# The first loads of an encoder kernel, cut in another way and in another order

## The chip, the cores and the metric

The kernel runs on one core of one Trainium2 chip. The metric is the time on the device in microseconds (us) of one execution. Before the change it is 922.29 us, the median of three runs (920.82 to 923.38).

The engines are named as in the profile: PE multiplies matrices (PEld loads its stationary operand), DVE and ACT work on vectors, POOL does small work, SP issues the transfers from memory. Each engine takes its instructions strictly in the order of its own queue.

## The reference

Two layers of an encoder for 256 rows (`SEQ`) of 1024 columns, in float32. The start of the first layer is all that the change touches:

```python
u = rms_norm(h, g_mix_pre)                       # h is the input x in layer 0
(gq, gk, gv, gg, ra_f, ra_b, aq, ak, av, gate_a, gate_b) = jnp.split(u @ w_in, offsets, axis=-1)
```

The rest of a layer is gated linear attention, grouped-query attention with rotary positions, a merge of both, a SwiGLU block and an embedding. The first columns that the kernel multiplies are the 32 decay ranks (`ra_f`, `ra_b`) and the 1024 of `aq`, which lie side by side in `w_in`: 1056 columns.

## The kernel before

**Numbers in two parts.** Each operand is cut into a high part (a copy in the format that PE takes at full rate) and the low remainder. A product is three matmuls: high by high, low by high, and high by the remainder of the weights. ACT makes the high part of a weight by a copy, DVE makes the remainder by a subtraction.

**K-tiles.** The 1024 columns of x are eight k-tiles of 128. For each, PE turns x (a transpose of 128x128 for each half of the rows, `turn`), then a high part (`high` on ACT or `high_here` on DVE) and a low part (`rest` on DVE) are made, scaled with the gain column `gcol`. The 1056 columns of weights are cut into 288, 384 and 384 (`RQ`), and each of these three and each half of the rows has its own accumulator: 18 matmuls for one k-tile. `rq_first` (the first four k-tiles, whose matmuls have line 105 in the profile) and `rq_step` (the others, line 121) issue them. For the very first k-tile the order is by column group, both halves in turn: four matmuls on the first 288 columns, four on the next 384, four on the last 384, then the six with the remainders of the weights.

**Loads.** SP issues x in pieces (`load_x`) and the weights by a list (`plan`, carried out by `Stream.load`). One load of the list holds two k-tiles, and there are two buffers for such loads; a load into a buffer waits until DVE has made the last remainder from it. `FIRST` says how the first two loads are cut: k-tile 0 as 288 and 768 columns, k-tile 1 whole, then k-tiles 2 and 3 whole. The order on SP is: x columns 0 to 256, the 288, the 768, k-tile 1, x columns 256 to 512, k-tiles 2 and 3, x columns 512 to 1024. The load of k-tiles 4 and 5 follows when its buffer is free, and behind it six small transfers of the decay weights (`up_weights`).

**The start.** `start()` is a generator that writes out the order by hand: `on(engine, ...)` chains its instructions on each engine, and `yield n` hands over to the matmuls for n steps (`tick`). In the kernel before, it turns k-tiles 0 and 1 of both halves (four transposes), issues two warm-up matmuls (`WARM[2]`), makes the high parts of k-tile 0 on DVE, then weights and low parts of k-tiles 0 and 1, and yields 5 steps before the turns of k-tiles 2 and 3. Work outside this list (line 774: ACT's copy of the decay weights, line 129: DVE's subtraction for it) is placed by a scheduler. Before any of it, PE runs six narrow and three wide warm-up matmuls (`WARM[0]`, `WARM[1]`) on constants.

In the profile all that `on` issues has line 142.

Of the kernel before, what the change touches and what calls it, by code (L numbers as in the profile page):

```python
# [48 lines left out]
UNIT = 2112  # L49
RQ = ((0, 288), (288, 672), (672, 1056))  # L50

WARM = 6, 3, 2

FIRST = ((0, 0, 288), (0, 288, 1056), (1, 0, 1056)), ((0, 0, 1056), (1, 0, 1056))
C_GQ, C_GK, C_GV, C_GG, C_RA = 0, 512, 1024, 2048, 3072
C_AQ, C_AK, C_GA, C_GB = 3104, 4128, 4640, 5664

# [2 lines left out]
def trunk_kernel(ctx: ExitStack, tc: tile.TileContext, a: dict, out: bass.AP):  # L60
# [21 lines left out]
    def nm(s):  # L82
        uid[0] += 1
        return f"{s}_{part[0]}_{uid[0]}"
# [10 lines left out]
    def aux():  # L95
        return accp.tile([P, 512], F32, tag="acc", name=nm("aux"))
# [7 lines left out]
    def mm(o, lhsT, rhs, start, stop):  # L104
        return nc.tensor.matmul(o, lhsT, rhs, start=start, stop=stop)  # L105

    def mm3(o, l, r, start, stop):
        (lh, ll), (rh, rl) = l, r
        mm(o, lh, rh, start, False)
        mm(o, lh, rl, False, False)  # L110
        mm(o, ll, rh, False, stop)
# [27 lines left out]
    def on(e, f, *args, **kw):  # L139

        with tc.issue_after(line[e].ins) if e in line else nullcontext():
            line[e] = f(*args, **kw)
# [9 lines left out]
    def load_x(c0, c1):  # L152
        on("dma", nc.sync.dma_start, h[:, :, c0:c1], a["x"][0, :, c0:c1].rearrange("(s p) c -> p s c", p=P))

    load_x(0, 256)
    on("act", nc.scalar.dma_start, grow, a["g_mix_pre"][0].rearrange("(k p) -> k p", p=P))


# [29 lines left out]
    def unit_rows(w, n, c0=0, c1=D, parts=None):  # L188

        if parts:  # L190

            return lambda t: [
                (t[:, k * (c1 - c0) + x : k * (c1 - c0) + y], w[(2 * n + k) * P : (2 * n + k + 1) * P, c0 + x : c0 + y])
                for k, x, y in parts
            ]
        return lambda t: [
            (
                t[:, : 2 * (c1 - c0)].rearrange("p (k c) -> p k c", k=2),
                w[n * 256 : (n + 1) * 256, c0:c1].rearrange("(k p) c -> p k c", p=P),
            )  # L200
        ]

    plan = []
    for l in range(DEPTH):
        w = a["w_in"][l]
        plan += [unit_rows(w, n, C_RA, C_RA + 1056, FIRST[n] if l == 0 and n < 2 else None) for n in range(4)]
        for c0 in (C_AK, C_GQ, C_GK, C_GV, C_GV + 512, C_GG, C_GG + 512):
# [25 lines left out]
    class Load:  # L233
# [5 lines left out]
        def start(self):  # L239
            if self.own:  # L240
                self.raw = self.own()
            else:
                self.raw = rawp.tile([P, UNIT], F32, tag="raw", name=nm("raw"))
            return self.make(self.raw)

    class Stream:
# [33 lines left out]
                self.lend = False  # L280
            return wp.tile([P, UNIT], F32R, tag=tag, name=nm("lent")).bitcast(F32)

        def load(self):

            self.room += 1
            self.start()

        def start(self):
            while self.loads and (self.lend or not self.loads[0].waits) and (self.loads[0].own or self.room):
                x = self.loads.pop(0)  # L290
                self.room -= not x.own
                moves = x.start()
                for dst, src in moves:
                    if self.open:
                        nc.sync.dma_start(dst, src)
                    else:
                        on("dma", nc.sync.dma_start, dst, src)
                x.n = sum(math.prod(dst.shape[1:]) for dst, _ in moves)
# [66 lines left out]
    ws = Stream(4)  # L365
# [410 lines left out]
        return wup  # L776


    ws.load()
    load_x(256, 512)  # L780
    ws.load()
    load_x(512, 1024)
    unit_a, unit_b = ws.pieces()
# [3 lines left out]
    def warm_up(n, wide=False):  # L787

        x = keep if wide else seed
        for _ in range(n):  # L790
            on("pe", mm, warm[:, 0 : x.shape[-1]], seed, x, True, True)

    warm_up(WARM[0])
    warm_up(WARM[1], True)
    uT = Split()
# [9 lines left out]
    def square_here(hf, j):  # L805
        on("dve", nc.vector.scalar_tensor_tensor, out=t512(), in0=hv(hf, j), scalar=1.0 / 1024.0, in1=hv(hf, j),
           op0=ALU.mult, op1=ALU.mult, accum_out=ss[hf][:, j : j + 1])

    def square(hf, j):
        on("act", nc.scalar.activation, t512(), hv(hf, j), AF.Square, scale=1.0 / 32.0, accum_out=ss[hf][:, j : j + 1])  # L810

    def rstd(hf):
        on("pool", nc.gpsimd.tensor_scalar,
           out=rs[hf], in0=ss[hf][:, 0:1], scalar1=ss[hf][:, 1:2], scalar2=EPS, op0=ALU.add, op1=ALU.add)
        on("pool", nc.gpsimd.tensor_scalar, out=he[hf], in0=rs[hf], scalar1=P * EPS, scalar2=None, op0=ALU.mult)
        on("pool", nc.gpsimd.tensor_tensor, out=rs[hf], in0=rs[hf], in1=neghalf[:, 0:1], op=ALU.pow)
        last_pow[0] = line["pool"]
# [10 lines left out]
    def gains():  # L828

        ps = aux()  # L830
        on("pe", nc.tensor.transpose, ps[:, 0:8], grow, ident[0:8, 0:8])
        on("dve", nc.vector.tensor_copy, gcol, ps[:, 0:8])

    def low(hi, lo, src):
        on("dve", nc.vector.tensor_tensor, out=lo, in0=src, in1=hi.bitcast(F32), op=ALU.subtract)

    def split_here(hi, lo, src):
        on("act", nc.scalar.copy, hi, src)
        low(hi, lo, src)
# [3 lines left out]
    def turn(hf, *ks):  # L843

        if (hf, ks[0] // 4) not in banks:
            banks[hf, ks[0] // 4] = aux()
        for k in ks:
            ps = banks[hf, k // 4][:, k % 4 * P : (k % 4 + 1) * P]
            on("pe", nc.tensor.transpose, ps, h[:, hf, k * P : (k + 1) * P], ident)

    def high(hf, *ks):

        for k in ks:
            ps = banks[hf, k // 4][:, k % 4 * P : (k % 4 + 1) * P]
            on("act", nc.scalar.activation, uT.at(k, 1, hf * P, P)[0][:, 0, :], ps, AF.Copy, bias=0.0, scale=gcol[:, k : k + 1])

    def high_here(hf, k):

        ps = banks[hf, k // 4][:, k % 4 * P : (k % 4 + 1) * P]
        hi = uT.at(k, 1, hf * P, P)[0][:, 0, :]  # L860
        on("dve", nc.vector.tensor_scalar, out=hi, in0=ps, scalar1=gcol[:, k : k + 1], scalar2=None, op0=ALU.mult)

    def rest(hf, *ks):

        for k in ks:
            ps = banks[hf, k // 4][:, k % 4 * P : (k % 4 + 1) * P]
            hi, lo = (t[:, 0, :] for t in uT.at(k, 1, hf * P, P))
            on("dve", nc.vector.scalar_tensor_tensor, out=lo, in0=ps, scalar=gcol[:, k : k + 1],
               in1=hi.bitcast(F32), op0=ALU.mult, op1=ALU.subtract)

    def start():
        cut = lambda piece, c: [t[:, c] for t in piece]

        def split_cut(piece):
            for c in RQ:
                on("act", nc.scalar.copy, *(t[:, slice(*c)] for t in piece[::2]))

        gains()
        for k in range(2):
            for hf in range(2):  # L880
                turn(hf, k)
        warm_up(WARM[2])
        for hf in range(2):
            high_here(hf, 0)
        split_cut(unit_a)
        rest(0, 0)
        rest(1, 0)
        low(*cut(unit_a, slice(0, 288)))
        for hf in range(2):
            high_here(hf, 1)  # L890
        low(*cut(unit_a, slice(288, 1056)))
        split_cut(unit_b)
        rest(0, 1)
        rest(1, 1)
        low(*cut(unit_b, slice(0, 288)))
        low(*cut(unit_b, slice(288, 1056)))
        ws.load()
        unit_c, unit_d = ws.pieces()
        yield 5
        turn(0, 2, 3)  # L900
        high(0, 2, 3)
        rest(0, 2, 3)
        split_here(*unit_c)
        yield 1
        turn(1, 2, 3)
        high(1, 2, 3)
        rest(1, 2, 3)
        yield 2
        split_here(*unit_d)
        ws.load()  # L910
        for hf in range(2):
            square(hf, 0)
        yield 3
        turn(0, 4, 5, 6, 7)
        for hf in range(2):
            square_here(hf, 1)
            rstd(hf)
        scales()
        ropes_first.extend(rope_tables(0))
        high(0, 4, 5, 6, 7)  # L920
        rest(0, 4, 5, 6, 7)
        yield 1
        turn(1, 4, 5, 6, 7)
        high(1, 4, 5, 6, 7)
        rest(1, 4, 5, 6, 7)
        for piece in ws.pieces():
            split_here(*piece)
        ws.load()
        ws.open = True
        ws.fill()  # L930
# [53 lines left out]
    for l in range(DEPTH):  # L984
# [258 lines left out]
        for x in range(2):  # L1243
            o = project_t(uT)
            for i in range(2):
                dst = qk[:, x, 2 * i : 2 * i + 2, :]
                src = o[i].rearrange("p (h t) -> p h t", t=T)
# [140 lines left out]
        for j in range(2):  # L1388
            o = project(uT)
            for hf in range(2):  # L1390
                dst = gg[:, hf, j * 512 : (j + 1) * 512]
# [210 lines left out]
        for x in FFN:  # L1602
# [3 lines left out]
            if x == "o":  # L1606
                n, w = outs.pop(0), ws.take()
# [115 lines left out]
```

## Time and profile before

| | before |
|---|---|
| median of 3 runs | 922.29 us |
| profiled execution | 922.96 us, span 921.2 us |
| PE busy | 911.5 us, 99% of the span |
| DVE, ACT busy | 85%, 63% |
| moved by DMA | 173.44 MB, 188 GB/s on average |

The span runs from the first to the last instruction of the profiled execution; its time is measured around it. A row in order of time gives the start in us, the length, the engine, the line, the operation with output and inputs, a count, and, in brackets, the idle time ahead of it with what ended it. Rows of several instructions start with the first; matmuls overlap, so the time per matmul is read from the starts of two rows.

### The profile page before, as it was taken

How to read it: one execution, taken by the hardware profiler on the slowest of the kernel's cores; microseconds unless marked ns; L12 is line 12 of the kernel's file. 1: busy time of each engine (PE TensorE's matmuls, PEld its weight loads, DVE VectorE, ACT ScalarE, POOL GpSimd, SP SyncE). 2: the span in 40 equal slices, each digit the busy share in tenths (PEclk: the TensorE clock that was granted, in tenths of full speed). 3: DMA queues.
4: the chain of work that ended last, by engine and by line, in shares of the span. 5: the costliest groups of instructions: out<-in, count | busy, mean ns of one | idle time of the engine just before them, and what ended most of it. 6: DMA issues, size and time to landing. Idle time of an engine off the chain costs nothing.

```text
span 921.2 us, 12422 instructions
## 1 busy us (share of the span) xinstructions
PE 911.5 (99%) x4669; PEld 778.3 (84%) x4669; DVE 786.2 (85%) x1009; ACT 581.4 (63%) x966; POOL 92.7 (10%) x149
## 2 busy tenths in 40 slices
PE   9999999999999999999999999999999999999996
PEld 8998888888888888888899988888888788888886
DVE  6988989987679998999779789798875799989875
ACT  5688667564567566566676677765644766565563
POOL 2710212210000000000114001100001000000000
PEclk9999999999999999999999999999999999999999
DMA  8663445657385655647576424454673856555361
GB/s 266 187 225 114 160 140 189 198 198 231 105 291 196 198 213 186 248 146 254 198 252 218 149 92 138 137 196 170 197 259 102 274 173 212 215 173 222 120 246 46
DMA packets 89079, 173.44 MB, mean 188 GB/s; under 512 B 3438, under 2 KB 27126, under 8 KB 88508
## 3 DMA queue, kind: packets, MB, share of 16 engines
q1 hardware_dynamic: 88860, 172.53, 55.8%
q8 instruction: 36, 0.59, 0.3%
q14 instruction: 23, 0.19, 0.1%
q10 hardware_dynamic: 160, 0.14, 0.0%
HBM read 169.50 MB, written 3.15 MB: 187 GB/s over the span
## 4 chain that ended last, share of the span: by engine, by line
PE 94%; DVE 2%; ACT 1%; DMA 1%; issue 1%; POOL 1%; SPq 0%; POOLq 0%; DVEq 0%; ACTq 0%
PE acc_0ffnin L121 12%; PE acc_1ffnin L121 11%; PE acc_1gate L121 7%; PE acc_0gate L121 7%; PE acc_0ffnin L105 7%; PE acc_1ffnin L105 7%; PE acc_1rq L121 3%; PE acc_0gqk L121 2%; PE acc_0wout L121 2%; PE acc_1gqk L121 2%; PE acc_0ple L121 2%; PE acc_1gg L121 2%; PE acc_0v L121 2%; PE acc_1merge L121 2%; PE acc_0merge L121 2%; PE acc_1ple L121 2%
## 5 line engine op out<-in xcount | busy, mean ns | idle before, releaser
L105 PE MATMUL acc_0ffnin<-wh_0ffnin,big_0ffnin 128*128 128x512 f32 x176 | 57.0, 393 | 0.0
L105 PE MATMUL acc_1ffnin<-wh_1ffnin,big_1ffnin 128*128 128x512 f32 x176 | 56.9, 392 | 0.0
L133 ACT CAST wh_1ffnin<-raw_1ffnin 128x1024 fp32r<-128x1024 f32 x38 | 38.5, 1050 | 27.2 <-PE acc_1ffnin L121 7.8
L133 ACT CAST wh_0ffnin<-raw_0ffnin 128x1024 fp32r<-128x1024 f32 x38 | 38.4, 1047 | 24.2 <-PE acc_0ffnin L121 7.9
L133 DVE TENSOR_TENSOR wl_1ffnin<-raw_1ffnin,wh_1ffnin 128x1024 fp32r<-128x1024 f32 x38 | 44.9, 1220 | 9.3 <-ACT wh_1ffnin L133 9.3
L133 DVE TENSOR_TENSOR wl_0ffnin<-raw_0ffnin,wh_0ffnin 128x1024 fp32r<-128x1024 f32 x38 | 44.8, 1220 | 7.6 <-ACT wh_0ffnin L133 7.5
L121 PE MATMUL acc_1ffnin<-wh_1ffnin,big_1wout 128*128 128x512 f32 x168 | 42.5, 393 | 0.0
L121 PE MATMUL acc_0ffnin<-wh_0ffnin,big_0wout 128*128 128x512 f32 x168 | 42.4, 393 | 0.0
L105 PEld LDWEIGHTS acc_0ffnin<-wh_0ffnin,big_0ffnin 128*128 128x128 f32 x176 | 33.0, 188 | 7.1 <-DVE big_0ffnin L133 0.4
L105 PEld LDWEIGHTS acc_1ffnin<-wh_1ffnin,big_1ffnin 128*128 128x128 f32 x176 | 33.0, 188 | 6.8
L133 DVE TENSOR_TENSOR wl_1ffnin<-lent_1ffnin,wh_1ffnin 128x1024 fp32r<-128x1024 f32 x30 | 35.8, 1216 | 1.7 <-ACT wh_1ffnin L133 1.7
L133 DVE TENSOR_TENSOR wl_0ffnin<-lent_0ffnin,wh_0ffnin 128x1024 fp32r<-128x1024 f32 x30 | 35.7, 1216 | 1.7 <-ACT wh_0ffnin L133 1.7
L121 PEld LDWEIGHTS acc_1ffnin<-wh_1ffnin,big_1wout 128*128 128x128 f32 x168 | 31.1, 188 | 6.2
L121 PEld LDWEIGHTS acc_0ffnin<-wh_0ffnin,big_0wout 128*128 128x128 f32 x168 | 31.1, 188 | 6.2
L133 ACT CAST wh_1ffnin<-lent_1ffnin 128x1024 fp32r<-128x1024 f32 x30 | 30.7, 1052 | 7.7 <-PE acc_1ffnin L105 3.9
L133 ACT CAST wh_0ffnin<-lent_0ffnin 128x1024 fp32r<-128x1024 f32 x30 | 30.7, 1053 | 7.0 <-PE acc_0ffnin L105 3.9
L105 PE MATMUL acc_1ffnin<-wl_1ffnin,big_1ffnin 128*128 128x512 f32 x88 | 34.4, 391 | 0.0
L105 PE MATMUL acc_0ffnin<-wl_0ffnin,big_0ffnin 128*128 128x512 f32 x88 | 34.3, 390 | 0.0
L133 DVE TENSOR_TENSOR wl_0gate<-raw_0gate,wh_0gate 128x1024 fp32r<-128x1024 f32 x20 | 24.2, 1254 | 5.3 <-ACT wh_0gate L133 5.2
L133 DVE TENSOR_TENSOR wl_1gate<-raw_1gate,wh_1gate 128x1024 fp32r<-128x1024 f32 x20 | 23.6, 1218 | 5.5 <-ACT wh_1gate L133 5.4
L133 ACT CAST wh_0gate<-raw_0gate 128x1024 fp32r<-128x1024 f32 x20 | 20.0, 1049 | 12.5 <-DMA raw_0gate<-in_w_o_attn_dram 6.1
L133 ACT CAST wh_1gate<-raw_1gate 128x1024 fp32r<-128x1024 f32 x20 | 20.1, 1050 | 12.1 <-DMA raw_1gate<-in_w_o_attn_dram 5.7
(711 smaller groups left out, 2704.9 us busy)
## 6 DMA issues: line engine op xcount, KB each, us to landing
raw_0ffnin<-in_w_ffn_out_dram SPq DMA_DIRECT2D x11, 1024.0 KB, 5.8
raw_1ffnin<-in_w_ffn_out_dram SPq DMA_DIRECT2D x11, 1024.0 KB, 6.1
lent_0ffnin<-in_w_ffn_in_dram SPq DMA_DIRECT2D x6, 1024.0 KB, 7.6
lent_1ffnin<-in_w_ffn_in_dram SPq DMA_DIRECT2D x6, 1024.0 KB, 8.1
raw_0v<-in_w_in_dram SPq DMA_DIRECT2D x4, 1024.0 KB, 5.0
raw_0gate<-in_w_o_gla_dram SPq DMA_DIRECT2D x4, 1024.0 KB, 5.2
raw_0gate<-in_w_o_attn_dram SPq DMA_DIRECT2D x4, 1024.0 KB, 5.1
raw_0wout<-in_w_ffn_in_dram SPq DMA_DIRECT2D x8, 512.0 KB, 5.2
```

Of the source, the lines that this page charges most:

```text
L105: return nc.tensor.matmul(o, lhsT, rhs, start=start, stop=stop)
L121: nc.tensor.matmul(o, x, y, start=start and n == 0, stop=stop and n == len(seq) - 1, **kw)
L133: return nc.scalar.copy(hi, src), nc.vector.tensor_tensor(out=lo, in0=src, in1=hi.bitcast(F32), op=ALU.subtract)
```

## The change

It does five things. x columns 0 to 128 come first instead of 0 to 256, and the other 128 come behind the weights of k-tile 0. These weights are cut into 672 and 384 columns instead of 288 and 768. The turns of k-tile 1 stand eight matmuls later, behind a `yield 2`; the yield after them goes from 5 to 4. For half 0 the high parts of k-tiles 0 and 1 are made by ACT (`high`) instead of DVE (`high_here`). Five instead of two warm-up matmuls stand behind the first turns. `load` gets an argument, a transfer to issue ahead of its n-th piece.

```diff
-WARM = 6, 3, 2
-FIRST = ((0, 0, 288), (0, 288, 1056), (1, 0, 1056)), ((0, 0, 1056), (1, 0, 1056))
+WARM = 6, 3, 5
+FIRST = ((0, 0, 672), (0, 672, 1056), (1, 0, 1056)), ((0, 0, 1056), (1, 0, 1056))
...
-    load_x(0, 256)
+    load_x(0, 128)
...
-                for dst, src in moves:
+                for n, (dst, src) in enumerate(moves):
+                    ahead.get(n, lambda: None)()
...
-    ws.load()
+    ws.load({2: lambda: load_x(128, 256)})
     load_x(256, 512)
...
         gains()
-        for k in range(2):
-            for hf in range(2):
-                turn(hf, k)
+        for hf in range(2):
+            turn(hf, 0)
         warm_up(WARM[2])
-        for hf in range(2):
-            high_here(hf, 0)
+        high(0, 0)
+        high_here(1, 0)
         split_cut(unit_a)
         rest(0, 0)
         rest(1, 0)
         low(*cut(unit_a, slice(0, 288)))
+        low(*cut(unit_a, slice(288, 1056)))
+        yield 2
         for hf in range(2):
-            high_here(hf, 1)
-        low(*cut(unit_a, slice(288, 1056)))
+            turn(hf, 1)
+        high(0, 1)
+        high_here(1, 1)
         split_cut(unit_b)
...
         ws.load()
         unit_c, unit_d = ws.pieces()
-        yield 5
+        yield 4
         turn(0, 2, 3)
```

The first `yield` now comes before `start()` has issued the load of k-tiles 4 and 5. The six transfers of the decay weights, which the layer issues behind the last load issued so far, therefore stand ahead of that load on SP. In the built program ACT's copy of the decay weights stands after the first of the second four high parts of k-tiles 4 to 7 (before: after the weights of k-tiles 4 and 5), and DVE's subtraction for it ahead of the second four low parts (before: after the remainders of k-tiles 4 and 5). The turns of k-tiles 2 and 3 stand six matmuls later in the order of PE, those of k-tiles 4 to 7 three later.

More of the change, by code (lines that the diff above doesn't have):

```diff
@@ L281, in lent, with load, start @@
             return wp.tile([P, UNIT], F32R, tag=tag, name=nm("lent")).bitcast(F32)
-        def load(self):
+        def load(self, ahead={}):
             self.room += 1
-            self.start()
-        def start(self):
+            self.start(ahead)
+        def start(self, ahead={}):
             while self.loads and (self.lend or not self.loads[0].waits) and (self.loads[0].own or self.room):
```

## The prediction

> **What bounds the kernel now.** I read the page first, then PE's busy time by stretch, PE's waits, the chain of waits at the start, and each engine's rows in order of time for the first 30 us.
>
> ```profile
> span 921.2 us, 12422 instructions
> ## 1 busy us (share of the span) xinstructions
> PE 911.5 (99%) x4669; PEld 778.3 (84%) x4669; DVE 786.2 (85%) x1009; ACT 581.4 (63%) x966; POOL 92.7 (10%) x149
> ```
>
> PE's busy time by stretch:
>
> ```profile
> 5.00:7.00 2.00, 1.32 (x5) 1.00 (x5) 1.53 (x6) 0.58 (x2) 0.00 (x0) 1.00 1.01 339
> 7.00:10.00 3.00, 3.00 (x10) 3.00 (x11) 2.63 (x5) 1.60 (x4) 0.00 (x0) 1.00 1.01 381
> ...
> 100.00:900.00 800.00, 799.35 (x3985) 675.73 (x3984) 691.31 (x834) 503.20 (x787) 59.76 (x99) 1.00 0.57 192
> ```
>
> PE's waits in the first 60 us, then pieces of the chain that ended last:
>
> ```profile
> PE acc_0rq L105 <- ACT wh_start L142: 0.7, 1, 0.7
> ```
>
> ```profile
> 1.79 4.60 DMA raw_start<-in_w_in_dram
> ...
> 33.95 5.23 PE acc_0kv L121 x23
> ```
>
> PE decides nearly everything: from 7 us on it is never out of work, and between 100 and 900 us it idles for 0.65. Its last wait at the start is the 0.7 us before the 384-column matmuls, behind a transfer. So a microsecond that PE gains or loses in the first 30 us should arrive whole at the end. PE's rows (start, length, operation, count):
>
> ```profile
> 3.58 1.11 PE L142 MATMUL aux_start<-ident,h 128*128 128x128 f32 x4 [0.23 <-DMA h<-in_x_dram]
> 4.49 0.42 PE L105 MATMUL warm<-seed 128*128 128x128 bf16 x2
> 5.01 1.30 PE L105 MATMUL acc_0rq<-wh_start,big_start 128*128 128x288 f32 x4
> 6.98 2.93 PE L105 MATMUL acc_0rq<-wh_start,big_start 128*128 128x384 f32 x8 [0.67 <-ACT wh_start L142]
> 9.71 1.96 PE L105 MATMUL acc_0rq<-wl_start,big_start 128*128 128x288 f32 x6
> 11.46 0.63 PE L142 MATMUL aux_start<-ident,h 128*128 128x128 f32 x2
> 11.75 1.57 PE L105 MATMUL acc_0rq<-wh_start,big_start 128*128 128x288 f32 x6
> 13.16 0.38 PE L142 MATMUL aux_start<-ident,h 128*128 128x128 f32 x2
> ...
> 15.30 2.08 PE L105 MATMUL acc_0rq<-wh_start,big_start 128*128 128x288 f32 x12
> 17.22 0.60 PE L142 MATMUL aux_start<-ident,h 128*128 128x128 f32 x4
> 17.57 0.72 PE L105 MATMUL acc_0rq<-wl_start,big_start 128*128 128x288 f32 x3
> 18.13 0.60 PE L142 MATMUL aux_start<-ident,h 128*128 128x128 f32 x4
> 18.48 0.73 PE L105 MATMUL acc_0rq<-wl_start,big_start 128*128 128x288 f32 x3
> 19.05 2.10 PE L105 MATMUL acc_0rq<-wh_start,big_start 128*128 128x288 f32 x12
> 20.98 1.13 PE L105 MATMUL acc_0rq<-wl_start,big_start 128*128 128x288 f32 x6
> 21.95 1.04 PE L121 MATMUL acc_0rq<-wh_start,big_start 128*128 128x288 f32 x6
> ```
>
> The pace is the second thing to see. Eight 384-column matmuls take 6.98 to 9.71, 0.34 us each; twelve (four of 288 columns, eight of 384) take 15.30 to 17.22, 0.16 each. PE runs at about half pace first. Six take 11.75 to 13.16, 0.235 each, between the two, so the full clock came at about 12.5 (estimate), some 5.5 us after PE's last idle gap. The clock column shows 1.00 all along; here the pace is the witness.
>
> **The change part by part.** The sum is made against the profiled execution (922.96 us, 1.8 of it around the span), which stands 0.67 above the median of 922.29.
>
> *First loads.* Transfers at the start, with KB and us to landing, and ACT's first copies:
>
> ```profile
> h<-in_x_dram SPq DMA_DIRECT2D x1, 256.0 KB, 2.7
> raw_start<-in_w_in_dram SPq DMA_DIRECT2D x1, 144.0 KB, 2.6
> raw_start<-in_w_in_dram SPq DMA_DIRECT2D x1, 384.0 KB, 4.6
> ```
>
> ```profile
> 3.92 0.43 ACT L142 CAST wh_start<-raw_start 128x288 fp32r<-128x288 f32 x1 [1.20 <-DMA raw_start<-in_w_in_dram]
> 6.42 0.92 ACT L142 CAST wh_start<-raw_start 128x384 fp32r<-128x384 f32 x2 [2.06 <-DMA raw_start<-in_w_in_dram]
> 7.80 1.26 ACT L142 CAST wh_start<-raw_start 128x288 fp32r<-128x288 f32 x3 [0.46 <-DMA raw_start<-in_w_in_dram]
> ```
>
> In KB up to its end, the 288-column copy could start at 3.92 after 256+144 = 400, the next at 6.42 after 784. The 672 columns end at 128+336 = 464 KB: by straight line 4.34. The upper end is 6.42. I take 4.95, above the line because the queue was slow just there (384 KB in 2.5 us) and nearer the lower row in bytes. With 0.43 for the copy and 0.1 to PE the first real matmul starts at 5.5 (4.9 to 6.95), not 5.01. In exchange the 0.7 us wait goes: the second group of columns has its weights with the first transfer; the third, and the second piece of x, end at 656 and 784 KB, the latter the row at 6.42, and PE wants them some 2.2 us after its start, at 7.7. By 6.98 PE has then done 1.48 us of slow work against 1.0 (four of 0.25, 0.34 by 288/384), but the two transposes of the second k-tile (0.23 each, four in 3.58 to 4.49) now stand in the stream: 1.48 - 1.0 - 0.46, nothing gained: **0**.
>
> *Clock.* PE is unbroken from 5.5 instead of 6.98. If the clock comes the same 5.5 us later, it comes 1.48 us earlier, and slow time is half lost: **-0.74**. Ends: 0 if it doesn't move, about -1.7 if it moves to 9.1.
>
> [...]
>
> *Three more warm-up matmuls*, 0.1 us each (4.49, two before the next row at 5.01 with its wait): they fill the time in which PE waits for the 672 columns. Hidden; 0.3 if those came at the lower end. *High part of half 0 moved from DVE to ACT*: the two run side by side while the weights travel; 0. *One more issue on SP* (0.45): later transfers are wanted microseconds after landing; 0. *Turns of k-tiles 2 and 3* stand six matmuls later: from them to k-tile 2 PE had 3.84 us (11.46 to 15.30), at full pace it will have about 2.2, and ACT needs as much (0.63 to its start, two high parts of 0.25, a copy of 1.05); 0, at most 0.3.
>
> *Turns later, copy of the decay weights earlier.* The scheduler's order of the changed program shows the second group of waits. The decay weights' six small transfers now precede the load of k-tiles 4 and 5, so ACT's copy (L774) stands inside the second four high parts and DVE's subtraction (L129) ahead of half 1's low parts; before, both came behind. ACT, then DVE, now:
>
> ```profile
> 17.85 2.18 ACT L142 ACTIVATE big_start<-aux_start,gcol_start 128x128 fp32r<-128x128 f32 x8 [1.41 <-PE aux_start L142]
> 19.87 2.10 ACT L142 CAST wh_start<-raw_start 128x1056 fp32r<-128x1056 f32 x2
> 21.81 1.08 ACT L774 CAST mid_0rq<-mid_start 81x1024 fp32r<-81x1024 f32 x1
> ```
>
> ```profile
> 19.04 2.16 DVE L142 SCALAR_TENSOR_TENSOR big_start<-aux_start,gcol_start,big_start 128x128 fp32r<-128x128 f32 x8 [0.77 <-ACT big_start L142]
> 21.11 2.42 DVE L142 TENSOR_TENSOR wl_start<-raw_start,wh_start 128x1056 fp32r<-128x1056 f32 x2
> 23.56 1.22 DVE L129 TENSOR_TENSOR mid_0rq<-mid_start,mid_0rq 17x1024 fp32r<-17x1024 f32 x1
> ```
>
> Count from the first four-transpose group. ACT: 0.63 to its first high part (17.22 to 17.85), 2.0 for eight, 0.95 to 1.05 for the copy, 1.05 for k-tile 4: ready at 4.7. PE, whose group stands three matmuls later: 0.35+0.56+0.35, then 18 matmuls in 2.90 (19.05 to 21.95): there at 4.16, where it had 4.73 before. It waits 0.5. DVE: the copy is done at about 3.0, the subtraction at 4.2, four low parts at 5.3, then 1.2 for each weight remainder: 6.5 and 7.7. PE, started at 4.7, wants the first after nine matmuls (6.15) and the second seven later: 0.4 and 0.1 more. Together **+1.0** (0 if ACT and DVE find slack; 2.3 if copy and subtraction, 1.08+1.22, lie whole on the path). I take the count.
>
> *Load of k-tiles 4 and 5* waits for a transfer ahead of it and is issued some 1 us later than its 10.11 row; its copy is wanted at about 20:
>
> ```profile
> 10.11 0.38 SPq L142 DMA_DIRECT2D raw_start<-in_w_in_dram  x1
> ```
>
> Hidden; 1 if that cover were gone.
>
> Sum: 0 - 0.74 + 1.0 = +0.26, so 923.2 for the profiled execution and 922.5 at the median.
>
> **The rivals.** *A clock that doesn't move* (PE's first idle stretch is now longer, about 1.2 us before 5.5, and PE may count as idle for it): +1.0, 923.3. *Late 672 columns*, the slower side: if they land with today's second transfer (6.42), PE loses its 1.0+0.46 of slow work (0.7 at full pace), gets no earlier clock, and still waits: +1.7, 924.0. Each microsecond more costs one; slower by over 0.3% (2.8 us, about what a measurement here tells from no change) needs a first matmul at about 8, a copy start near the 7.80 row. For it: a 336 KB piece is nearer to 384 than to 144. Against it: less is queued ahead. *No new waits*: if ACT and DVE keep up at k-tiles 4 and 5, -0.74, 921.5; with the clock at 9.1, 920.5. For it: ACT idled 1.41 us before 17.85; against: that idling is a wait for PE.
>
> *A clock on a grid of its own.* The runs shown span 920.82 to 923.38 with one program. If the full clock comes only at marks that don't start with the kernel, the same early start gets it anywhere within a stretch like the 2.7 us between 9.8 and 12.5, half of that in time, and the median can come out at 921.4 or at 923.6 with all else right. [...] One execution can't show it.
>
> **How the numbers follow.** Forecast 922.5 (own range 921.8 to 923.2): 0.34. Clock unmoved, 923.3: 0.18. Late columns, 924 and up: 0.18. No waits, 921.5 or less: 0.18. The grid, at either of its ends: 0.1. The rest 0.02. The range from 920.6 to 924.8 leaves out the far ends of the late columns and of no waits. Faster by over 0.3% takes both an early clock and no waits: 0.08; slower takes columns later than any row: 0.16; within: 0.76, since every other case lies nearer than 2.8 us.
>
> **What would show it.** In the changed kernel's rows: first real matmul near 5.5 and no gap until k-tile 4; pace falling from 0.34 to 0.17 at about 11 rather than 12.5; PE waits on ACT's copy of k-tile 4 (0.5) and on DVE's remainders (0.5); the 0.7 us wait gone. The prediction is wrong if a gap opens between the first and the third group, if the pace changes after 12.5, or if a wait of over a microsecond stands anywhere after 30 us.

## The result, and the profile after

The changed kernel takes 923.78 us (median of 21 runs, 921.95 to 925.37); the kernel before, run beside it, 922.03 (median of 21, 920.76 to 923.38). The ratio is 1.0018, with a 95% interval of 1.0011 to 1.0025: 1.75 us slower, inside the 0.3% that were called no change, and 1.3 us over the forecast of 922.5, above that forecast's own range of 921.8 to 923.2. The profiled execution lies near the median: 923.82 us, span 922.1.

The page of the changed kernel, its first line, PE's share and the chain that ended last; the same chain line of the kernel before stands behind it:

```profile
span 922.1 us, 12432 instructions
...
PE 911.0 (99%) x4672; PEld 777.0 (84%) x4672; DVE 784.8 (85%) x1007; ACT 582.5 (63%) x968; POOL 90.9 (10%) x149
...
PE 84%; DVE 6%; ACT 3%; DMA 3%; issue 2%; POOL 1%; SPq 0%; POOLq 0%; DVEq 0%; ACTq 0%
```

```profile
PE 94%; DVE 2%; ACT 1%; DMA 1%; issue 1%; POOL 1%; SPq 0%; POOLq 0%; DVEq 0%; ACTq 0%
```

PE works as long as before (911.0 against 911.5) in a span that is 0.9 longer; the chain is off PE for 16% of the span instead of 6%. Where it leaves PE is the question.

PE's rows of the changed kernel at the start (start, length, operation, count, idle time and what ended it):

```profile
3.76 0.74 PE L105 MATMUL warm<-seed 128*128 128x128 bf16 x5
5.26 2.61 PE L105 MATMUL acc_0rq<-wh_start,big_start 128*128 128x288 f32 x8 [0.76 <-ACT wh_start L142]
7.67 0.63 PE L142 MATMUL aux_start<-ident,h 128*128 128x128 f32 x2
7.95 1.31 PE L105 MATMUL acc_0rq<-wh_start,big_start 128*128 128x384 f32 x4
9.10 1.12 PE L105 MATMUL acc_0rq<-wl_start,big_start 128*128 128x288 f32 x6
...
19.18 1.13 PE L105 MATMUL acc_0rq<-wl_start,big_start 128*128 128x288 f32 x6
20.64 1.63 PE L121 MATMUL acc_0rq<-wh_start,big_start 128*128 128x288 f32 x9 [0.33 <-ACT wh_start L142]
22.46 0.40 PE L121 MATMUL acc_0rq<-wl_start,big_start 128*128 128x288 f32 x1 [0.19 <-DVE wl_start L142]
...
24.89 0.86 PE L121 MATMUL acc_0rq<-wh_start,big_start 128*128 128x384 f32 x4
...
32.95 2.07 PE L121 MATMUL acc_0kv<-wh_start,big_start 128*128 128x512 f32 x8
```

Two of the same places in the kernel before:

```profile
25.63 0.87 PE L121 MATMUL acc_0rq<-wh_start,big_start 128*128 128x384 f32 x4
...
33.71 2.07 PE L121 MATMUL acc_0kv<-wh_start,big_start 128*128 128x512 f32 x8
```

The last six matmuls of k-tiles 2 and 3 start at 19.18 (20.98 before): PE is 1.80 us ahead. At the four 384-column matmuls of k-tiles 4 and 5 shown, 24.89 against 25.63, only 0.74 is left, and 0.76 arrives at the keys and values (32.95 against 33.71). The waits in between, 0.33 and 0.19, are on what the prediction named: ACT's copy and DVE's remainder.

At 57 us the rest is lost. ACT's rows of the changed kernel, then of the kernel before:

```profile
53.79 0.60 ACT L1252 ACTIVATE big_0gqk<-acc_0gqk 128x512 f32<-128x512 f32 x1 [0.36 <-PE acc_0gqk L121]
54.74 2.00 ACT L133 CAST wh_0kv<-raw_0rq 128x1024 fp32r<-128x1024 f32 x2 [0.35 <-DMA raw_0rq<-in_w_in_dram]
56.65 0.57 ACT L133 CAST mid_0at<-aux_0at 128x512 fp32r<-128x512 f32 x1
57.12 0.37 ACT L133 CAST big_0kv<-aux_0kv 128x256 fp32r<-128x256 f32 x1
58.33 0.60 ACT L1252 ACTIVATE big_0gqk<-acc_0gqk 128x512 f32<-128x512 f32 x1 [0.83 <-PE acc_0gqk L121]
```

```profile
54.93 0.58 ACT L133 CAST mid_0at<-aux_0at 128x512 fp32r<-128x512 f32 x1
55.40 0.39 ACT L133 CAST big_0kv<-aux_0kv 128x256 fp32r<-128x256 f32 x1
55.66 2.02 ACT L133 CAST wh_0kv<-raw_0rq 128x1024 fp32r<-128x1024 f32 x2
58.20 0.60 ACT L1249 ACTIVATE big_0gqk<-acc_0gqk 128x512 f32<-128x512 f32 x1 [0.52 <-PE acc_0gqk L121]
```

The cast of a weight unit (wh_0kv) has moved ahead of the casts of the queries (mid_0at) and of the keys (big_0kv); it waits for its load, and those two wait behind it (PE's matmuls into aux_0at, the input of mid_0at, end at 54.19, and ACT idles from 54.39 to 54.74). PE feels it, and the chain of waits between 50 and 62 us, which was PE alone in the kernel before, runs through that load:

```profile
57.55 0.51 PE L105 MATMUL aux_0at<-big_0kv,mid_0at 128*128 128x256 f32 x2 [0.51 <-ACT big_0kv L133]
```

```profile
49.58 5.14 DMA raw_0rq<-in_w_in_dram
54.72 0.02 issue
54.74 2.00 ACT wh_0kv L133 x2
56.74 0.48 ACT mid_0at L133
57.22 0.28 ACT big_0kv L133
```

ACT's second copy of big_0gqk starts at 58.33 against 58.20: the 0.76 of lead has become 0.13 of lag. Neither the change's diff nor its text touches this place; the order there is the scheduler's.

How much is lost depends on the load. In three other kernels with the same order of casts (e_warm, e_after9 and e_upearly, described below) the load has landed, the cast starts without a wait, and PE loses 0.40, 0.40 and 0.45 us here. This is the cast's row in e_warm:

```profile
54.91 1.99 ACT L133 CAST wh_0kv<-raw_0rq 128x1024 fp32r<-128x1024 f32 x2
```

In the two profiles of the changed kernel, where the cast waits 0.35 and 0.54 us for its load, PE loses 0.88 and 1.06.

A third loss stands at the start of layer 1 (474 us). ACT's row there, PE's wait and ACT's row after it, in the changed kernel; then ACT's two rows in the kernel before:

```profile
469.04 2.06 ACT L133 CAST wh_0ple<-raw_0ple 128x1056 fp32r<-128x1056 f32 x2 [1.43 <-DMA raw_0ple<-in_w_in_dram]
...
474.70 1.32 PE L445 MATMUL aux_0ple<-ident,mid_0ple 128*128 128x128 f32 x8 [0.32 <-DVE mid_0ple L515]
...
481.47 2.00 ACT L133 CAST wh_1rq<-raw_0ple 128x1024 fp32r<-128x1024 f32 x2 [3.85 <-PE acc_1rq L121]
```

```profile
467.68 2.06 ACT L133 CAST wh_0ple<-raw_0ple 128x1056 fp32r<-128x1056 f32 x2 [0.18 <-DMA raw_0ple<-in_w_in_dram]
...
480.65 2.00 ACT L133 CAST wh_1rq<-raw_0ple 128x1024 fp32r<-128x1024 f32 x2 [4.38 <-PE acc_1rq L121]
```

A weight load lands about a microsecond late, ACT stands still for it, PE then waits for DVE, and 0.1 of lag becomes 0.82.

### The profile page after: what moved, and what is told of

It reads as the page before. It is cut to its first block, busy times and chain, and to the rows that moved or that the text cites. A ratio compares the mean times of both kernels' runs of the same rounds, so it can differ in the third digit from the quotient of the medians.

```text
span 922.1 us, 12432 instructions
## 1 busy us (share of the span) xinstructions
PE 911.0 (99%) x4672; PEld 777.0 (84%) x4672; DVE 784.8 (85%) x1007; ACT 582.5 (63%) x968; POOL 90.9 (10%) x149
## 4 chain that ended last, share of the span: by engine, by line
PE 84%; DVE 6%; ACT 3%; DMA 3%; issue 2%; POOL 1%; SPq 0%; POOLq 0%; DVEq 0%; ACTq 0%
PE acc_1ffnin L121 11%; PE acc_0ffnin L121 11%; PE acc_0gate L121 7%; PE acc_1gate L121 7%; PE acc_1ffnin L105 7%; PE acc_0ffnin L105 6%; PE acc_0wout L121 2%; PE acc_1gqk L121 2%; PE acc_1gg L121 2%; PE acc_0v L121 2%; PE acc_0merge L121 2%; PE acc_1merge L121 2%; PE acc_1ple L121 2%; PE acc_0gg L121 2%; PE acc_1rq L121 2%
```

## The experiments

The first four runs separate the start (first loads, turns, warm-ups) from the place of the decay weights (`up_weights`: the six transfers, ACT's copy and DVE's subtraction), and look at the two losses that this place brings. Each run stands beside runs of the kernel before that were made with it.

**The decay weights late again (e_up).** The changed kernel, with `up_weights(0)` called inside `start()` behind the load of k-tiles 4 and 5:

```diff
         unit_c, unit_d = ws.pieces()
+        with tc.issue_after(line["dma"].ins):
+            wup_first.append(up_weights(0))
         yield 4
...
-            with after_start:
-                wup = up_weights(0)
```

> The changed kernel with one thing put back: layer 0's up-weights (six DMAs, the copy on ACT, the subtraction on DVE) come behind the load of k-tiles 4 and 5 again, as in the kernel before; first loads, warm-ups and turns stay as the change has them. ACT, DVE and SP then go in the order of the kernel before from k-tile 2 on. Theory 1: the change gains 0.2 to 1.9 us by its first 18 us and loses about 1.0 us at k-tiles 4 and 5 (up-weights ahead) and about 0.9 us at 57 us (the weight cast of ACT ahead of the casts of q and of the keys, an order that the early up-weights bring). Both losses go here: 0.2 to 1.9 us under the kernel before, 920.1 to 921.8. Rival 2: the start itself costs, on the mean over executions, because full pace mostly comes no earlier; then it stays near the changed kernel, 923 to 924.

Measured: 921.95 us (11 runs) beside 921.96 for the kernel before (33 runs), ratio 1.0000 (0.9991 to 1.0009). Both losses go (PE keeps 0.83 us of lead from 24 to 264 us), and so do 1.8 us of the time. But nothing is gained over the kernel before: theory 1's 0.2 to 1.9 us under it did not come. The profile loses 0.7 at 268 us and 0.8 at 474 us, so the lead did not reach the end.

ACT's rows of e_up at the two places, in the order of the kernel before:

```profile
17.25 2.17 ACT L142 ACTIVATE big_start<-aux_start,gcol_start 128x128 fp32r<-128x128 f32 x8 [0.76 <-PE aux_start L142]
19.26 2.10 ACT L142 CAST wh_start<-raw_start 128x1056 fp32r<-128x1056 f32 x2
21.21 1.07 ACT L775 CAST mid_start<-mid_start 81x1024 fp32r<-81x1024 f32 x1
...
54.10 0.58 ACT L133 CAST mid_0at<-aux_0at 128x512 fp32r<-128x512 f32 x1
54.57 0.39 ACT L133 CAST big_0kv<-aux_0kv 128x256 fp32r<-128x256 f32 x1
54.83 2.02 ACT L133 CAST wh_0kv<-raw_0rq 128x1024 fp32r<-128x1024 f32 x2
```

**The decay weights early, alone (e_upearly).** The kernel before, with the same call ahead of that load:

```diff
+        with tc.issue_after(line["dma"].ins):
+            wup_first.append(up_weights(0))
+        line["dma"] = last_up[0]
         ws.load()
         unit_c, unit_d = ws.pieces()
```

> The kernel before with that one thing alone: the up-weights come ahead of the load of k-tiles 4 and 5; first loads, warm-ups and turns stay as in the kernel before. ACT and DVE then go in the order of the changed kernel from k-tile 4 on. Theory 1: it pays both losses without the gain, 1.0 + 0.9 = 1.9 us over the kernel before, 923.9. Rival 2 (the start costs, the up-weights do not): equal to the kernel before, 922.0, within 0.5.

Measured: 923.85 beside 921.96, ratio 1.0023 (1.0013 to 1.0033). The decay weights in another place (six small transfers, with the copy and the subtraction that the scheduler moves along) cost as much as the whole change. In its profile PE loses 1.07 us at k-tiles 4 and 5, most of it in one wait on DVE's remainder, and 0.45 at 57 us, together 1.5. Rival 2 falls.

```profile
23.31 0.40 PE L121 MATMUL acc_0rq<-wl_start,big_start 128*128 128x288 f32 x1 [0.70 <-DVE wl_start L142]
```

**The order at 57 us alone (e_act).** The changed kernel; the one unit whose cast got ahead is held until the keys' second half is cast:

```diff
                 n = self.total - len(self.jobs)
+                if n == 9 and not behind_keys and not must:
+                    break
...
+                if l == 0 and hf == 1:
+                    behind_keys.append(made[0])
+                    with tc.issue_after(made[0].ins):
+                        ws.fill()
```

> The changed kernel, up-weights early as the change has them, but the cast of the one weight unit that got ahead at 54 us is held on ACT behind the cast of the keys' second half. Theory 1: the wait of 0.5 us of PE on big_0kv at 57 us goes, and with it the 0.9 us that PE's lead lost there: 922.9. Rival 3: that wait is covered by another that ends at the same time (the matmuls that have to wait for the weights instead), so that the time stays at 923.8.

Measured: 922.87 beside 921.96, ratio 1.0009 (0.9999 to 1.0019): 0.9 under the changed kernel, as expected, and 0.9 over the kernel before, which leaves the losses at k-tiles 4 and 5 and at 474 us. The two medians are from different sets of runs, and the interval reaches 1.0 us to either side, so the size is rough. Its profile has no wait on big_0kv any more, but still loses 0.35 us between 48 and 66, with no row that names it. That is nearly what e_warm, e_after9 and e_upearly lose there with the new order and no wait for the load. So the profiles show the order of the casts as the cause only of the part that comes with that wait, about half; the cause of the other half is open.

**The three added warm-ups (e_warm).** `WARM = 6, 3, 2` in the changed kernel.

> The changed kernel with two warm-up matmuls behind the first turns in place of five, as in the kernel before. Theory 1: three of 0.1 to 0.2 us each lie in a stretch in which PE waits for the first weights anyway; time within 0.4 us of the changed kernel, 923.4 to 924.2. Rival 4: they fill a gap that else delays full pace; then full pace comes later by 1 us or more and the time is 0.5 us or more over the changed kernel, 924.3 or above.

Measured: 923.40 beside 921.96, ratio 1.0012 (1.0003 to 1.0021), at theory 1's lower end; full pace at 10.1. So no cost of the three shows at the start; what they do elsewhere comes below.

The next runs ask what the start itself is worth.

**The later turns alone (e_turns).** The kernel before with the changed `start()`, its own cuts of x and weights, two warm-ups, decay weights late.

> The kernel before with the later turns alone: the columns of x and the weights come in the cuts of the kernel before, two warm-ups as before, up-weights late as before, but the second k-tile's turns stand behind the first twelve matmuls. Theory 1: first matmul still at about 5.0, the wait of 0.7 us at 6.98 stays or grows, full pace as in the kernel before; 921.5 to 922.5. Rival 2: the turns alone cost because the second k-tile's high and low parts come later on DVE and ACT; a wait of PE between 8 and 12 us, 922.6 or above.

Measured: 922.16 beside 922.42, ratio 1.0000 (0.9991 to 1.0010). No cost, as theory 1 has it. The turns wait 0.70 us for x, the first real matmul starts at 5.30 after another 0.35, and the wait at 6.98 is gone, not kept as expected. So the later turns remove that wait even with the old cuts of x and weights; what the new cuts add to that, no run shows.

**More warm-ups with the decay weights late (e_up9).** e_up with `WARM = 6, 3, 9`.

> The changed first loads and turns with the up-weights late again, as in e_up, and nine warm-up matmuls behind the first turns in place of five: they should fill most of the 0.8 to 1.0 us that PE waits there for the first weights. Theory 1a (full pace is granted a set time after PE became busy without a pause): full pace comes before 8 us in place of 9.9, PE is 0.7 us or more further ahead, and the time is 0.5 to 1.5 us under e_up: 920.5 to 921.5. Rival 1b (full pace is granted on a grid of its own, wherever PE's pauses lie): no change to e_up beyond chance, 921.9, or 0.2 more where the last warm-ups delay the first matmuls.

Measured: 921.13 beside 922.42, ratio 0.9987 (0.9978 to 0.9996). Full pace came at 8.95, so the mechanism of theory 1a (pace before 8) isn't what was seen, though the time was in its range.

**Both kernels once more (before_again, after_again).** One profiled execution each, nothing changed.

> The kernel before once more, for its profile: whether full pace at 12.5 us is what it mostly has (theory: no, it lies anywhere between 10 and 13), and whether the weight load at 467 us and the matmuls at 57 us are as in the first profile.

> The changed kernel once more, for its profile. Theory 1: the loss of 1.0 us at k-tiles 4 and 5 and the wait on big_0kv at 57 us are there again; full pace comes between 8.5 and 10.5 us, and the loss of 0.7 us at 474 us is there in some executions only.

Measured: 922.54 with full pace at 11.1, and 924.46 with full pace at 8.7. The changed kernel loses 1.07 us at k-tiles 4 and 5 again, 1.06 at 57 us (its wait on big_0kv is now 0.70) and 0.62 at 474 us: all three are there again, the last against the expectation that it comes only at times.

**Repeats, and the remaining combinations (e_up_b, e_up9_b, e_after9, e_up11).** e_up and e_up9 unchanged; the changed kernel with `WARM = 6, 3, 9`; e_up with `WARM = 6, 3, 11`.

> e_up once more, beside the same runs of the kernel before as the nine warm-ups: its first profile kept 0.8 us of lead over the kernel before from 24 us to 260 us and lost 0.7 us at 268 us and 0.8 us at 474 us. If these two losses are chance, the profile mostly has none of them and the median stands 0.3 to 1.0 us under the kernel before; if they belong to the kernel, they are there again and the median is that of the kernel before.

> e_up9 once more. If its gain is real: 0.8 to 1.8 us under the kernel before, and under e_up_b by 0.4 us or more. If it was chance: equal to e_up_b.

> The changed kernel, up-weights early as the change has them, with nine warm-ups in place of five. Theory 5: with the early up-weights a lead from the start does not pass 57 us, because there the casts of q and of the keys stand behind a weight cast that waits for its load, and the load lands at about 54.8 whatever PE's lead is; so nothing comes of the gain: 923.3 to 924.0, PE's wait on big_0kv at 57 us 0.5 us or more. Rival 6 (the terms only add): the 0.8 to 1.3 us that the nine warm-ups brought come through, 922.5 to 923.0.

> The up-weights late and eleven warm-ups in place of nine, so that PE's last pause ahead of the first real matmuls (0.19 us with nine) goes. If any pause puts full pace off: pace before 8.0 us and 0.3 us or more under the version with nine. If pauses so short do not matter: full pace at 8.5 to 9.5 and the time of the version with nine, up to 0.2 us more where the warm-ups push the first matmuls back.

Measured, beside 921.88 (33 runs): e_up_b 922.35, ratio 1.0003 (0.9994 to 1.0011); e_up9_b 921.53, 0.9997 (0.9987 to 1.0007); e_after9 922.39, 1.0005 (0.9994 to 1.0016); e_up11 921.54, 0.9999 (0.9990 to 1.0007). So e_up equals the kernel before. The gain of e_up9 shrinks from 1.29 to 0.35: whether late decay weights with nine or eleven warm-ups beat the kernel before by a few tenths is undecided, and most of the first run's 1.29 did not come again. For e_after9 theory 5 falls: 922.39 lies under its 923.3, 1.4 us under the changed kernel. In its profile the last packet of the load in question ended at 54.12 (54.32 in the changed kernel), and ACT didn't wait for it. e_up11 doesn't test what it was made for: the first weights came later there, the first matmul started at 5.49 and a pause of 0.35 stayed.

Why should four matmuls at 4 us be worth 1.4 us? Here are all profiles side by side. Full pace is where the trace's record of the full granted clock starts. PE's lead is the median difference of the start of the same matmuls to the first profile of the kernel before, over 6 us each (negative: ahead); the last two columns are the idle time that ACT's row at 467 us shows for its load, and whether the instruction transfer spoken of below overlaps that load by 0.9 us or more:

| kernel (warm-ups) | full pace at | lead at 18 | at 30 | at 66 | at 468 | at 486 | at the end | ACT's wait at 467 | overlap |
|---|---|---|---|---|---|---|---|---|---|
| before (2) | 12.5 | 0 | 0 | 0 | 0 | 0 | 0 | 0.18 | no |
| before_again (2) | 11.1 | -0.56 | -0.56 | -0.56 | -0.48 | -0.46 | -0.44 | 0.19 | no |
| e_upearly (2) | 11.0 | -0.97 | +0.10 | +0.55 | +0.50 | +0.52 | +0.47 | 0.17 | no |
| e_turns (2) | 10.4 | -1.01 | -0.76 | -0.76 | -0.77 | -0.78 | -0.74 | 0.31 | no |
| e_warm (2) | 10.1 | -1.18 | -0.13 | +0.27 | +0.23 | +0.23 | +0.49 | 0.33 | no |
| after (5) | 8.8 | -1.80 | -0.76 | +0.12 | +0.10 | +0.82 | +0.89 | 1.43 | yes |
| after_again (5) | 8.7 | -1.89 | -0.82 | +0.24 | +0.29 | +0.91 | +1.55 | 1.36 | yes |
| e_act (5) | 10.5 | -1.12 | -0.10 | +0.25 | +0.20 | +0.63 | +0.07 | 1.14 | yes |
| e_up (5) | 9.9 | -1.08 | -0.83 | -0.83 | -0.24 | +0.58 | 0.00 | 1.53 | yes |
| e_up_b (5) | 8.6 | -2.00 | -1.76 | -1.76 | -1.78 | -0.90 | -0.43 | 1.58 | yes |
| e_after9 (9) | 9.7 | -1.47 | -0.42 | -0.02 | -0.08 | -0.09 | -0.53 | 0.16 | no |
| e_up9 (9) | 9.0 | -1.82 | -1.58 | -1.58 | -1.56 | -1.56 | -1.24 | 0.27 | no |
| e_up9_b (9) | 4.5 | -2.94 | -1.13 | -1.13 | -1.21 | -1.20 | -1.32 | 0.33 | no |
| e_up11 (11) | 9.9 | -1.13 | -0.92 | -0.92 | -0.97 | -0.98 | -1.52 | 0.25 | no |

All five profiles of kernels with five warm-ups, and none of the nine others, lose 0.4 to 0.9 us between 468 and 486 and have ACT wait over 1.1 us at 467. Of the 1.4 us between the changed kernel and e_after9, 0.72 stands there and 0.48 at 57 us (0.88 against 0.40). The lead changes once more between 876 and 892 us, by up to 0.7 us, up in some profiles and down in others; that was not traced to a cause.

The transfers tell more about 467 us. Queue q8, which the trace marks as instruction, moves packets of 16 KB (36 of them in the kernel before, and as many in the changed one); one such packet is called the fetch here. These two lines, of the changed kernel between 467 and 468 us and of e_after9 between 462 and 464, give packets, MB and share of 16 engines:

```profile
q8 instruction: 1, 0.02, 5.9%
```

```profile
q8 instruction: 1, 0.02, 2.9%
```

By the trace's packets the load starts at 463.75 in the changed kernel and the fetch at 467.02, inside it, 0.95 us long (5.9% of 16 engines over 1 us); the load's last packets then come after 468. In e_after9 the fetch runs from 463.09 to 464.02 and the load from 463.57 to 467.23; ACT starts right behind it:

```profile
467.59 2.06 ACT L133 CAST wh_0ple<-raw_0ple 128x1056 fp32r<-128x1056 f32 x2 [0.16 <-DMA raw_0ple<-in_w_in_dram]
```

With two warm-ups the fetch falls at the load's very end (467.17 against 467.24 in the kernel before). Over all profiles the two overlap by 0.92 to 1.36 us in the five, and the load of 1 MB then takes 4.5 to 4.9 us; in the nine others they overlap by 0.53 at most, and it takes 3.6 to 3.8. The count of warm-ups was the only edit between after, e_warm and e_after9, and between e_up, e_up9 and e_up11; why the fetch comes at another time with another count was not shown. That the fetch holds up the load is read from the coincidence in 14 of 14 profiles; the fetch was not moved by itself. In the five in which it falls into this load, PE's lead falls by 0.4 to 0.9 us.

## Why the prediction was right or wrong

*First matmul at 5.5, no gap until k-tile 4*: right. It starts at 5.26 (4.98 to 5.61 in the five other profiles with these loads and two or five warm-ups), and the 0.67 at 6.98 is gone. The rival of late columns, whose 924.0 lies nearest to the measured time, is ruled out all the same: the weights were there.

*Clock, -0.74*: right in direction and near in size, but not by the mechanism given. Full pace came at 8.6 to 10.5 in the six profiles with the new loads and two or five warm-ups, at 11.0 to 12.5 in the three with the old start: earlier in every one. PE's lead at 18 us is -1.51 on the mean of the six (-1.80, -1.89, -1.12, -1.08, -2.00, -1.18) against -0.51 of the three (0, -0.56, -0.97), a gain of 1.0 us. e_turns, with the old loads and the later turns alone, has 10.4 and -1.01, so the gain can't be put down to the new loads.

The set delay of 5.5 us after the last pause, from which 0.74 came, isn't one: from PE's start after its last shown pause it was 3.5 in after (5.26 to 8.8), 5.6 in the kernel before (6.98 to 12.5), and in e_up9_b full pace came ahead of the first real matmul, at 4.5, which is 3.4 us after PE's first warm-up at 1.05. The rival of a grid of its own fits the instant better. The traces keep the granted clock as records (ahead of the first, where none stands, the views print 1.00). The record of full clock lasts 904.53 us in the kernel before and 911.36 in the changed kernel, and in each of the 14 profiles 904.53, 907.95 or 911.36, three values 3.42 and 3.41 us apart. Its start differs between profiles of one kernel (12.5 and 11.1, 8.8 and 8.7, 9.9 and 8.6, 9.0 and 4.5), and with it PE's lead at 18 us, by 0.1 to 1.1 us. The rival's marks would explain both; the marks themselves stand in no trace. The rival's prices were rough: it took a stretch of 2.7 us, and its two ends, 921.4 and 923.6, lie further apart than half of that. No trace gives the 9.1 us of the term's early end either; three of the six came before it (8.6, 8.7 and 8.8). Why -0.74 came near all the same was not shown: PE's last pause ends at 5.0 to 5.6 in the six and at 6.4 to 7.1 in the three, and full pace comes earlier in the six, but by no set delay.

Nor did transposes in the slow stretch keep full pace away: two at 7.67 in the changed kernel (full pace at 8.8), two at 11.46 in the kernel before (12.5), two at 3.28 in e_up9_b (4.5).

*Waits at k-tiles 4 and 5, +1.0*: right. In the six profiles with early decay weights the lead falls by 1.02 to 1.07 us there; with late ones and the new start by 0.21 to 0.25 (1.81 in e_up9_b, below). The rival of no new waits falls. The two parts agree as well. From 19.18 to 20.64 are 1.46 us, where the same six matmuls took 0.97 before (20.98 to 21.95): 0.49 for ACT's copy, predicted 0.5. From 20.64 to 22.46 are 1.82, where nine take 1.46 at 0.162 each (19.05 to 20.98, twelve in 1.93): 0.36 for DVE's first remainder, predicted 0.4. The rest, 0.2, stands behind it, predicted 0.1. The idle times in the rows, 0.33 and 0.19, show less than that, because the ends of matmuls are modelled.

*Three more warm-ups, 0*: right for the first 30 us; at 474 us every profile with five warm-ups loses 0.4 to 0.9. In the time of the kernel the three do not show (923.40 without them, 923.78 with them, and the intervals overlap).

*"So a microsecond that PE gains or loses in the first 30 us should arrive whole at the end"*: this is the step that failed. It holds where nothing in between changes (e_turns carries its 0.76 from 30 us to the end, 0.74), and it took every later place for unchanged. The decay weights' place changed the scheduler's order of ACT and PE at 57 us; at 467 us, by the coincidence above, an instruction fetch came under a load. The prediction looked at the new order only for the first 30 us. Its own test, a wait of over a microsecond after 30 us, did not see this on PE, whose waits there are 0.51 and 0.32; the long one stands on ACT, 1.43 us instead of 0.18.

The terms, from the leads: -1.0 by 18 us, +1.05 at k-tiles 4 and 5, +0.97 at 57 us (mean of 0.88 and 1.06), +0.67 at 474 us (0.72 and 0.62); together +1.7, where 1.75 was measured. So close an agreement is partly chance: the first term is a difference of means over several kernels, and the leads at the end give 1.44 (0.89 and 1.55 in the changed kernel against 0 and -0.44). Predicted were -0.74 and +1.0, and nothing behind. That the time still lies within the 0.3% is owed to the width of that range and to a start that gained a little more than forecast. The gain at the start is real by the profiles, but doesn't show in the median of e_up: in its two profiles it pays 0.25 at k-tiles 4 and 5 and 0.8 to 0.9 at 474 us, which leaves little or nothing (921.95 and 922.35 against 921.96 and 921.88).

*Load of k-tiles 4 and 5, hidden*: right where it was asked. In e_up9_b it is the bound: PE was so early (2.94 us ahead) that ACT waited for this load, and 1.8 us of the lead went.

```profile
19.03 2.05 ACT L142 CAST wh_start<-raw_start 128x1056 fp32r<-128x1056 f32 x2 [1.47 <-DMA raw_start<-in_w_in_dram]
```

What stays open: what the new loads bring beyond the later turns, the changes of the lead behind 876 us, the 0.35 to 0.45 us that every kernel with early decay weights loses near 57 us even without a wait for the load, the 0.7 us that e_up lost once at 268 us and e_up_b did not, and whether nine warm-ups with late decay weights beat the kernel before.

## What to carry to other kernels

When an edit lets a scheduler see another order, compare the whole new order with the old one on every engine, and not just the stretch of the edit: here six small transfers moved ahead of one load, with the copy and the subtraction behind them, cost 1.9 us, part of it 35 us further on. Put a transfer that nobody needs soon behind the load that the next matmuls need. And in a kernel that is 99% busy a gain at the start must be followed to the end, place by place, since any load-bound place on the way may take it back.

## What the runs showed of the hardware

In the five profiles in which a 16 KB instruction packet (0.92 to 1.44 us) overlapped a 1 MB weight load by 0.92 us or more, what waits for that load came about a microsecond later (ACT waits 1.14 to 1.58 instead of 0.16 to 0.33); kernels with three matmuls less or four more, 460 us earlier, did not have it. The record of full clock lasted 904.53, 907.95 or 911.36 us in the 14 profiles (904.53 in the kernel before, 911.36 in the changed kernel). Full pace came anywhere from 4.5 to 12.5 us over 14 profiles, and two profiles of the same kernel differ by up to 4.5 us (e_up9 and its repeat), so one profile of a start says little about its median.
